# Spreading the row factors of four norms: two one-pass products of their head and rest in place of one fp32 product

## The chip, the cores and the metric

The kernel runs on one core of one Trainium2 chip. The metric is the time of one execution on the device in microseconds (us); the median of three runs is 1458.67 us.

## The reference, cut to what matters

The network has two layers. Each layer normalises the 512 tokens of width 1024, projects them, mixes them in three branches, adds the result, normalises again and runs an MLP; a last norm closes the network.

```python
def rms_norm(x, g):
    xf = x.astype(F32)
    y = xf * lax.rsqrt(jnp.mean(xf * xf, axis=-1, keepdims=True) + EPS)
    return (y * g.astype(F32)).astype(x.dtype)

for l in range(DEPTH):                      # DEPTH = 2
    h = rms_norm(x, norm1_g[l])
    z = h @ w_in[l]
    ...                                     # three branches on slices of z, gated and summed
    x = x + merged @ w_out[l]
    h2 = rms_norm(x, norm2_g[l])
    x = x + jnp.square(jax.nn.relu(h2 @ w_ff1[l])) @ w_ff2[l]
return rms_norm(x, final_norm_g)
```

A row of the norm is multiplied by one factor per token, `rsqrt(mean(x*x) + EPS)`. The kernel does not multiply `h` by it; it multiplies the products of `h` by it later, and for products that have the tokens along the free axis it needs the 512 factors repeated on all 128 partitions.

## The kernel before

Tokens lie in NT = 4 tiles of 128, the width in KB = 8 blocks of 128. Every large product is made of three one-pass fp32r products: head by head, head by rest, rest by head (`mm3`, line 261). Activations in head and rest are `xgh`/`xgl` (after the first norm), `xq`, `xz`, `xy`, `xc` (in the MLP) and `sqh`/`sql` (the MLP's hidden values); weights come by DMA into `raw` (3 buffers), are cast to a head `wh` on ScalarE (ACT) and to a rest `wl` on VectorE (DVE) or on ACT and GpSimd (POOL).

`Norm.stats()` (line 349) makes the factors. From the sums of squares it makes `st_v`, POOL raises it to the power -0.5 into `st_r` (128 x 4: one column for each token tile). Where they are wanted on all partitions (`bc=True`), DVE makes a page `sq` (128 x 512) with four `tensor_scalar` instructions, `ident` times one column of `st_r` each, so four diagonal blocks. TensorE (PE) multiplies a 128 x 128 tile of ones with this page in one fp32 product `statb<-sq,ones` into a PSUM bank; each of its 512 columns then holds a token's factor on every partition. ACT copies the bank into the page `rbc`. Pages of the tag `sq` have two buffers, `rbc` has one.

This happens four times, named here **place 1 to 4**: at the start of layer 0 (line 1091, about 28 us), ahead of the MLP of layer 0 (line 1180, about 413 us), at the start of layer 1 (about 751 us) and ahead of its MLP (about 1127 us). `rbc` is read by DVE: in `s5_u` (line 666, `s5u<-mx,rbc`, the input of one branch, which then goes out to memory and back by the DMAs `bn<-s5u` and `u<-bn` of SP's queue), in `gate_tile` (line 1079), and at the MLP's entry in `fft<-mm,rbc`, which leads over `fft<-fft` to `sqh<-fft` on ACT and `sql<-fft,sqh` on DVE, the operands of the MLP's second product.

The order of instructions on each engine is not written out by hand. The Tile scheduler lays it out with a time simulation of its own at build time (line 1345), under the data dependences, the buffers' turns and some dependences that the kernel adds. An edit that changes a few instructions can so change the order of others around it. Every instruction is recorded at line 110, a wrapper; rows are told apart by the names of their tiles.

Of the kernel before, what the change touches and what calls it, by code (L numbers as in the profile page):

```python
# [10 lines left out]
F32 = dt.float32  # L11
F32R = dt.float32r
AF = mybir.ActivationFunctionType
ALU = mybir.AluOpType

P = 128
# [4 lines left out]
NT = SEQ // P  # L21
# [72 lines left out]
def build(tc, x, positions, norm1_g, w_in, lam_re, lam_im, log_step, b_re, b_im, c_re, c_im, ssm_d,  # L94
# [28 lines left out]
    pe, ve, sc, gp, sy = (Ordered(e) for e in (nc.tensor, nc.vector, nc.scalar, nc.gpsimd, nc.sync))  # L123
    es = contextlib.ExitStack()
    with es:
        cp = es.enter_context(tc.tile_pool(name="cst", bufs=1))
# [3 lines left out]
        def f(t):  # L130
            return t.bitcast(F32)

        def page(dtype=F32, name="pg", tag="pg"):
            t = pool.tile([P, 512], dtype, tag=tag, bufs=BUFS[tag], name=name)
            pending[t.tensor.name] = tag
            return t
# [10 lines left out]
        def small(n, name, bufs=2, dtype=F32):  # L147
            return pool.tile([P, n], dtype, tag=name, bufs=bufs, name=name)
# [4 lines left out]
        def mx_ps(name="mx"):  # L153
            return psp.tile([P, 512], F32, tag="mx", bufs=4, name=name)

        def copy(o, i, scale=1.0):
            sc.activation(o, i, AF.Copy, scale=scale)
# [19 lines left out]
        def cst(n):  # L177
            o, w = COFF[n]
            return ct[:, o:o + w]

        ident, tri, vis, iota, rep32 = (cst(n) for n in ("ident", "tri", "vis", "iota", "rep32"))
        ones = cp.tile([P, P], F32, name="ones")
        gp.memset(ones, 1.0)
        nhalf = cp.tile([P, 16], F32, name="nhalf")
        gp.memset(nhalf, -0.5)
# [112 lines left out]
        class Norm:  # L298
# [50 lines left out]
            def stats(self, bc=True, ts=range(NT)):  # L349
                v = small(NT, "st_v")  # L350
                tt = slice(ts[0], ts[-1] + 1)
                if self.sums is None:
                    ps = mx_ps("stat")
                    for t in ts:
                        pe.matmul(ps[:, 2 * t:2 * t + 2], self.acc[:, t * P:(t + 1) * P], ones[:, 0:2], start=True, stop=True)
                    sums = ps[:, 0:2 * NT].rearrange("p (t a) -> p t a", a=2)[:, tt, 0]
                else:
                    sums = self.sums[:, tt]
                ve.tensor_scalar(v[:, tt], sums, 1.0 / DM, EPS, op0=ALU.mult, op1=ALU.add)
                r = small(NT, "st_r")  # L360
                gp.tensor_tensor(r[:, tt], v[:, tt], nhalf[:, tt], ALU.pow)
                if not bc:
                    return r, None
                dg = page(name="sq", tag="sq")
                for t in range(NT):
                    ve.tensor_scalar(dg[:, t * P:(t + 1) * P], ident, r[:, t:t + 1], None, op0=ALU.mult)
                pb = mx_ps("statb")
                pe.matmul(pb, ones, dg, start=True, stop=True)
                rb = page(name="rbc", tag="rbc")
                copy(rb, pb)  # L370
                return r, rb
# [977 lines left out]
```

## Time and profile before

| | us |
|---|---|
| median of three runs (lowest to highest) | 1458.67 (1458.5 to 1458.79) |
| the profiled execution, its own time | 1458.82 |
| span of the profiled execution | 1456.9 |
| PE busy | 1435.8 |
| DVE busy | 1061.0 |
| ACT busy | 785.1 |
| POOL busy | 176.4 |

The profiled execution's own time is 1.9 us longer than its span, and 0.15 us over the median. The mean granted clock of PE is 0.997 of full speed. A matmul's row gives its start, its length from first column to modelled end, and its operands; neighbouring matmuls overlap, so what one occupies on PE is the distance between the starts, not the length. One fp32 `statb` instruction shows as two records.

### The profile page before, as it was taken

How to read it: one execution, taken by the hardware profiler on the slowest of the kernel's cores; microseconds unless marked ns; L12 is line 12 of the kernel's file. 1: busy time of each engine (PE TensorE's matmuls, PEld its weight loads, DVE VectorE, ACT ScalarE, POOL GpSimd, SP SyncE). 2: the span in 40 equal slices, each digit the busy share in tenths (PEclk: the TensorE clock that was granted, in tenths of full speed). 3: DMA queues.
4: the chain of work that ended last, by engine and by line, in shares of the span. 5: the costliest groups of instructions: out<-in, count | busy, mean ns of one | idle time of the engine just before them, and what ended most of it. 6: DMA issues, size and time to landing. Idle time of an engine off the chain costs nothing.

```text
span 1456.9 us, 22130 instructions
## 1 busy us (share of the span) xinstructions
PE 1435.8 (99%) x8102; PEld 1263.3 (87%) x8102; DVE 1061.0 (73%) x2448; ACT 785.1 (54%) x1224; POOL 176.4 (12%) x247
## 2 busy tenths in 40 slices
PE   8999999999999999999999999999999999999997
PEld 7889898888889889999889889888888999999996
DVE  6966799745877988877576479766477777677754
ACT  5654665663645555555545654566544454545454
POOL 0221121100010011100101112211100000000011
PEclk9999999999999999999999999999999999999999
DMA  7874775846245665655847757768542656565664
GB/s 230 198 151 103 175 174 137 198 102 181 87 113 150 152 155 156 153 144 138 205 148 172 182 125 162 180 140 179 145 149 81 151 153 152 152 152 153 152 162 128
DMA packets 164081, 222.82 MB, mean 153 GB/s; under 512 B 14906, under 2 KB 134532, under 8 KB 163972
## 3 DMA queue, kind: packets, MB, share of 16 engines
q1 hardware_dynamic: 140180, 142.69, 32.2%
q0 software_dynamic: 22464, 76.56, 28.4%
q10 hardware_dynamic: 1328, 2.17, 0.4%
q8 instruction: 63, 1.03, 0.3%
q14 instruction: 46, 0.38, 0.1%
HBM read 136.44 MB, written 8.39 MB: 99 GB/s over the span
## 4 chain that ended last, share of the span: by engine, by line
PE 89%; DMA 5%; issue 3%; DVE 2%; ACT 1%; POOL 0%; SPq 0%; POOLq 0%; ACTq 0%; DVEq 0%
PE mm L110 60%; PE f L110 18%; DMA raw<-in_w_in_dram 2%; DMA wl<-raw 2%; PE yo L110 1%; PE mx L110 1%; PE sp L110 1%; PE pv L110 1%; PE ry L110 1%; PE tr L110 1%; PE pt L110 1%; PE s5y L110 1%; DMA xt<-in_x_dram 1%; DMA raw<-in_w_ff_dram 1%; PE kk L110 0%
## 5 line engine op out<-in xcount | busy, mean ns | idle before, releaser
L110 ACT ACTIVATE wh<-raw 128x1024 fp32r<-128x1024 f32 (+3 forms) x314 | 306.2, 976 | 345.9 <-PE mm L110 219.3
L110 POOL DMA_DIRECT2D wl<-raw x156 | 136.5, 875 | 1002.8 <-ACT wl L110 557.3
L110 DVE TENSOR_TENSOR wl<-raw,wh 128x896 fp32r<-128x896 f32 (+3 forms) x158 | 171.3, 1085 | 92.2 <-ACT wh L110 91.7
L110 PE MATMUL f<-xc,wh 128*128 128x256 f32 x1232 | 224.6, 279 | 0.0
L110 ACT ACTIVATE wl<-raw 128x1024 fp32r<-128x1024 f32 (+1 forms) x156 | 155.6, 998 | 83.4 <-PE mm L110 34.4
L110 PEld LDWEIGHTS f<-xc,wh 128*128 128x128 f32 x1232 | 190.9, 188 | 2.4
L110 PE MATMUL mm<-sql,wh 128*128 128x512 f32 x480 | 188.2, 393 | 0.0
L110 PE MATMUL mm<-sqh,wl 128*128 128x512 f32 x480 | 187.5, 391 | 0.1
L110 PE MATMUL mm<-sqh,wh 128*128 128x512 f32 x480 | 185.1, 391 | 0.0
L110 PE MATMUL f<-xc,wl 128*128 128x256 f32 x616 | 170.3, 279 | 0.0
L110 PE MATMUL mm<-xgh,wh 128*128 128x512 f32 x384 | 151.5, 395 | 1.2 <-ACT zq L110 1.2
L110 PE MATMUL mm<-xgl,wh 128*128 128x512 f32 x384 | 151.7, 395 | 0.0
L110 PE MATMUL mm<-xgh,wl 128*128 128x512 f32 x384 | 151.3, 395 | 0.0
L110 DVE TENSOR_TENSOR raw<-raw 128x256 f32<-128x256 f32 x336 | 107.8, 334 | 52.5 <-DMA raw<-in_w_ff_dram 48.6
L110 PEld LDWEIGHTS f<-xc,wl 128*128 128x128 f32 x616 | 115.4, 188 | 0.5
L110 PE MATMUL mm<-wh,xgh 128*128 128x384 f32 (+1 forms) x320 | 106.1, 336 | 2.7 <-ACT wh L110 1.4
L110 PEld LDWEIGHTS mm<-sqh,wl 128*128 128x128 f32 x480 | 90.2, 188 | 19.6 <-DMA wl<-raw 0.5
L110 PE MATMUL mm<-wl,xgh 128*128 128x384 f32 (+1 forms) x320 | 105.8, 333 | 0.9 <-DVE wl L110 0.7
L110 PEld LDWEIGHTS mm<-sqh,wh 128*128 128x128 f32 x480 | 90.1, 188 | 17.9
L110 PEld LDWEIGHTS mm<-sql,wh 128*128 128x128 f32 x480 | 90.2, 188 | 17.1
L110 PE MATMUL mm<-wh,xgl 128*128 128x384 f32 (+1 forms) x320 | 102.7, 334 | 0.0
L110 DVE TENSOR_TENSOR x<-x,mm 128x512 f32<-128x512 f32 x120 | 80.9, 682 | 9.9 <-PE mm L110 9.9
(405 smaller groups left out, 2865.1 us busy)
## 6 DMA issues: line engine op xcount, KB each, us to landing
wl<-raw POOLq DMA_DIRECT2D x116, 512.0 KB, 5.3
raw<-in_w_ff_dram SPq DMA_DIRECT2D x72, 512.0 KB, 3.5
raw<-in_w_ff_dram SPq DMA_DIRECT2D x112, 256.0 KB, 2.8
raw<-in_w_in_dram SPq DMA_DIRECT2D x52, 512.0 KB, 4.9
wl<-raw POOLq DMA_DIRECT2D x40, 384.0 KB, 4.9
raw<-in_w_in_dram SPq DMA_DIRECT2D x32, 384.0 KB, 3.7
raw<-in_w_out_dram SPq DMA_DIRECT2D x16, 512.0 KB, 3.4
xd<-x SPq DMA_DIRECT2D x16, 256.0 KB, 3.5
```

What stands on the lines that cost most here:

```text
L110: r = fn(*a, **k)
```

## The change

The ones become a tile of type fp32r, and the factors are split on DVE into a head (`st_h`, rounded to fp32r) and a rest (`st_l`). Each part gets a diagonal page of type fp32r, and two one-pass products of the ones with these pages add up in the same PSUM bank.

```diff
-        ones = cp.tile([P, P], F32, name="ones")
+        ones_r = cp.tile([P, P], F32R, name="ones")
+        ones = f(ones_r)
         gp.memset(ones, 1.0)
...
                 if not bc:
                     return r, None
-                dg = page(name="sq", tag="sq")
-                for t in range(NT):
-                    ve.tensor_scalar(dg[:, t * P:(t + 1) * P], ident, r[:, t:t + 1], None, op0=ALU.mult)
+                rh, rl = small(NT, "st_h", 2, F32R), small(NT, "st_l")
+                ve.tensor_copy(rh, r)
+                ve.tensor_tensor(rl, r, f(rh), ALU.subtract)
                 pb = mx_ps("statb")
-                pe.matmul(pb, ones, dg, start=True, stop=True)
+                for n, y in enumerate((f(rh), rl)):
+                    dg = page(F32R, "sq", "sq")
+                    for t in range(NT):
+                        ve.tensor_scalar(dg[:, t * P:(t + 1) * P], ident, y[:, t:t + 1], None, op0=ALU.mult)
+                    pe.matmul(pb, ones_r, dg, start=n == 0, stop=n == 1)
                 rb = page(name="rbc", tag="rbc")
                 copy(rb, pb)
                 return r, rb
```

Over the whole program PE goes from 4 to 8 `statb` products and DVE gets 24 more instructions: 4 casts, 4 subtractions and 16 `tensor_scalar`. ACT, POOL and the DMA queues have the same instructions in number. The scheduler's order differs near the four places only.

On PE at place 1, before: the last products of a group of 128 x 292 outputs, then `statb`, then 48 products into `mx`.

```order
L110 MATMUL mm<-wh,xgl 128x292 [waits DVE_49]
L110 MATMUL mm<-wh,xgl 128x292 x3
L110 MATMUL statb<-sq,ones 128x512 [waits DVE_49,PE_49]
L110 MATMUL mx<-xgh,wh 128x512 [waits PE_49]
L110 MATMUL mx<-xgl,wh 128x512
```

On PE at place 1, now:

```order
L110 MATMUL mm<-wh,xgl 128x292 [waits DVE_49]
L110 MATMUL mm<-wh,xgl 128x292 x3
L110 MATMUL mm<-wh,xgh 128x384 [waits Activation_49]
L110 MATMUL mm<-wh,xgh 128x384 x2
L110 MATMUL statb<-sq,ones 128x512 [waits DVE_49,PE_49]
L110 MATMUL mx<-xgh,wh 128x512 [waits PE_49]
```

Three products of the next group (128 x 384 outputs), which stood behind the 48 of `mx`, now stand ahead of the first `statb`, and they wait for a weight head that ACT casts. The second `statb` stands behind 21 of the 48.

On SP's queue at place 1, before: the branch's input goes out to memory in two halves (`bn`), each read back by four DMAs (`u`), with one weight block (`raw`) ahead of the second four.

```order
L110 DMA bn_99<-s5u 128x512 [waits DMAHW6_49,DVE_49]
L110 DMA u<-bn_99 32x4x128 [waits DMAHW7_49,DMAHW6_49]
L110 DMA u<-bn_99 32x4x128
...
L110 DMA bn_100<-s5u 128x512 [waits DMAHW3_49,DVE_49]
L110 DMA raw<-in_w_in_dram 128x4x256 [waits DMAHW4_49,DVE_49]
L110 DMA u<-bn_100 32x4x128 [waits DMAHW5_49,DMAHW3_49]
```

On SP's queue at place 1, now:

```order
L110 DMA bn_99<-s5u 128x512 [waits DMAHW6_49,DVE_49]
L110 DMA bn_100<-s5u 128x512 [waits DMAHW7_49,DVE_49]
L110 DMA u<-bn_99 32x4x128 [waits DMAHW6_49]
...
L110 DMA u<-bn_100 32x4x128 [waits DMAHW7_49,DMAHW4_49]
L110 DMA u<-bn_100 32x4x128 [waits DMAHW5_49]
L110 DMA u<-bn_100 32x4x128 x2
L110 DMA raw<-in_w_in_dram 128x4x256 [waits DMAHW0_49,DVE_49]
```

The weight block moved behind all eight `u`.

On ACT at place 4 (place 2 reads alike), before: the copy to `rbc`, then the heads `sqh` of the MLP's hidden values in turn with casts of weights.

```order
L110 ACTIVATE rbc<-statb 128x512
L110 ACTIVATE sqh<-fft 128x512
L110 ACTIVATE wh<-raw 128x1024
L110 ACTIVATE sqh<-fft 128x512
L110 ACTIVATE wh<-raw 128x896
L110 ACTIVATE sqh<-fft 128x512
L110 ACTIVATE wh<-raw 128x896
L110 ACTIVATE sqh<-fft 128x512
L110 ACTIVATE wl<-raw 128x1024
```

On ACT at place 4, now:

```order
L110 ACTIVATE rbc<-statb 128x512
L110 ACTIVATE wh<-raw 128x1024
L110 ACTIVATE sqh<-fft 128x512 x2
L110 ACTIVATE wh<-raw 128x896 x2
L110 ACTIVATE wl<-raw 128x1024
L110 ACTIVATE sqh<-fft 128x512 x2
```

The casts of weights moved ahead of the heads: one ahead of the first pair, three ahead of the second.

## Rows read from the trace of the kernel before

**Rows 1.** The page's part 1: busy time, share and instructions of each engine

```profile
PE 1435.8 (99%) x8102; PEld 1263.3 (87%) x8102; DVE 1061.0 (73%) x2448; ACT 785.1 (54%) x1224; POOL 176.4 (12%) x247
```

**Rows 2.** Stretch: us, busy (count) PE PEld DVE ACT POOL, clock, DMA share, GB/s

```profile
745.00:760.00 15.00, 15.00 (x83) 13.06 (x84) 9.66 (x47) 5.95 (x12) 1.04 (x1) 1.00 0.37 104
1120.00:1142.00 22.00, 22.00 (x122) 18.79 (x121) 16.36 (x33) 9.46 (x12) 3.22 (x3) 1.00 0.42 112
```

**Rows 3.** Timeline of PE at place 1: start us, us, instruction, [idle before]

```profile
26.80 0.80 PE L110 MATMUL mm<-wh,xgl 128*128 128x292 f32 x4
27.68 1.10 PE L110 MATMUL statb<-sq,ones 128*128 128x512 f32 x2
...
28.85 0.40 PE L110 MATMUL mx<-xgl,wh 128*128 128x512 f32 x1
```

**Rows 4.** Timeline of PE 30 us later

```profile
57.48 0.34 PE L110 MATMUL mm<-wh,xgl 128*128 128x384 f32 x1
59.04 0.50 PE L110 MATMUL mm<-xgh,wh 128*128 128x512 f32 x1 [1.23 <-ACT zq L110]
```

**Rows 5.** The chain that ended last, in order of time, up to 59 us

```profile
43.16 3.52 DMA raw<-in_w_in_dram
...
49.91 7.53 DMA raw<-in_w_in_dram
```

**Rows 6.** Timeline of PE at place 4

```profile
1127.02 0.62 PE L110 MATMUL mm<-xc,wh 128*128 128x512 f32 x2
1127.48 1.02 PE L110 MATMUL statb<-sq,ones 128*128 128x512 f32 x2
...
1128.57 0.62 PE L110 MATMUL mm<-xc,wh 128*128 128x512 f32 x2
```

**Rows 7.** The tile statb: duration in ns min/median/max, first and last start

```profile
L110 PE MATMUL statb<-sq,ones x8: 590/592/667, 27.7 to 1127.9; 128*128 128x512 f32 x8
```

**Rows 8.** Timeline of DVE at place 4 and behind it

```profile
1122.14 0.87 DVE L110 TENSOR_SCALAR sq<-ct,st_r 128x128 f32<-128x128 f32 x4
1125.11 1.08 DVE L110 TENSOR_TENSOR raw<-raw 128x256 f32<-128x256 f32 x3 [2.09 <-DMA raw<-in_w_ff_dram]
...
1129.17 1.29 DVE L110 TENSOR_TENSOR fft<-mm,rbc 128x512 f32<-128x512 f32 x2 [1.42 <-ACT rbc L110]
```

**Rows 9.** Timeline of DVE elsewhere: a small cast to fp32r

```profile
43.02 0.17 DVE L110 CAST p_rh<-p_th 128x16 fp32r<-128x16 f32 x1
```

**Rows 10.** Timeline of ACT behind place 4

```profile
1137.06 0.96 ACT L110 ACTIVATE wh<-raw 128x896 fp32r<-128x896 f32 x1 [0.99 <-ACT sqh L110]
1137.92 0.61 ACT L110 ACTIVATE sqh<-fft 128x512 fp32r<-128x512 f32 x1
```

**Rows 11.** Timeline of PE where the MLP's second product starts

```profile
1136.93 0.39 PE L110 MATMUL mm<-sqh,wh 128*128 128x512 f32 x1
...
1140.14 0.73 PE L110 MATMUL f<-xc,wh 128*128 128x256 f32 x5
1140.71 0.39 PE L110 MATMUL f<-xc,wl 128*128 128x256 f32 x2
```

**Rows 12.** Timeline of ACT at place 1

```profile
28.48 0.86 ACT L110 ACTIVATE wh<-raw 128x768 fp32r<-128x768 f32 x1
```

**Rows 13.** Timeline of SP's queue behind place 1 (time at the queue's head)

```profile
42.68 0.38 SPq L110 DMA_DIRECT2D bn<-s5u  x1
43.16 0.40 SPq L110 DMA_DIRECT2D raw<-in_w_in_dram  x1
45.34 1.74 SPq L110 DMA_DIRECT2D u<-bn  x4
```

**Rows 14.** Busy time by stretch in the first 61 us (columns as Rows 2)

```profile
8.34:11.75 3.41, 1.87 (x12) 1.38 (x12) 2.52 (x4) 3.41 (x9) 0.00 (x0) 1.00 0.94 335
11.75:15.16 3.41, 3.41 (x16) 3.41 (x16) 2.47 (x6) 3.41 (x10) 0.00 (x0) 0.50 0.33 81
...
57.00:60.50 3.50, 2.27 (x11) 1.73 (x10) 2.21 (x12) 2.48 (x4) 1.36 (x3) 1.00 0.95 225
```

## The prediction

> **What bounds the kernel now.** I read the page's busy times first: PE is busy 1435.8 of 1456.9 us, DVE 1061.0, ACT 785.1 [rows 1]. So PE's sequence sets the time, and a change counts by what PE occupies and by where PE comes to wait. The table by stretch shows it at the places: PE is busy 15.00 of 15.00 us round place 3 and 22.00 of 22.00 round place 4, DVE 9.66 and 16.36, the DMA engines 0.37 and 0.42 [rows 2]. Place 2 has the same pattern as place 4, so its rows are not shown. Place 1, at 27.68 [rows 3], is different. It lies in the first 60 us, where PE meets weights that have just come. There PE waits 1.23 us at 59.04 for ACT's `zq` [rows 4]; the chain of work shows that a weight block issued at 49.91 and landing 7.53 us later, at 57.44, stands behind that wait, and before it another that SP issued at 43.16 [rows 5].
>
> **What the products save.** At place 4 two one-pass products of 128 x 512 start at 1127.02 and what follows starts at 1127.48, so one occupies 0.46 / 2 = 0.23 us of PE. From the start of `statb` at 1127.48 to 1128.57 lie the fp32 product and one such one-pass product: 1.09 us, so the fp32 product occupies 1.09 - 0.23 = 0.86 us [rows 6]. Two one-pass products occupy 0.46. Each place saves 0.40 us, four places 1.60. The eight records of `statb` last 590 to 667 ns with a median of 592, so the four places are alike [rows 7]; at place 1 the distance is 28.85 - 27.68 - 0.23 = 0.94, because PE waits a little inside it [rows 3].
>
> A rule of the Trainium skill would give a little more. "FP8 and Floating Point Precision", section TensorE Precision Notes, says that true fp32 takes four passes through the array. By it the old product would occupy 4 x 0.23 = 0.92 us, an estimate, each place would save 0.46, and the four 1.84 in place of 1.60; the row of place 4 has 0.86, and I go by the row.
>
> **What DVE pays at places 2, 3 and 4.** The four `tensor_scalar` of one diagonal take 0.87 us [rows 8]. The added diagonal costs that again, and the cast and the subtraction (128 x 4) at most the 0.17 us each that a cast of 128 x 16 lasts [rows 9]: at most 0.87 + 0.34 = 1.21 us a place. At place 4 DVE next waits 2.09 us for a DMA [rows 8], and at place 2 as well, so the addition lies wholly in that wait; without it, it would delay weight rests by 1.2 us. At place 3 no such single wait follows, but DVE is busy only 9.66 of 15.00 us in that stretch [rows 2], and the second `statb` stands ten products (2.3 us) behind the first, more than its diagonal takes. So on PE's path the split costs nothing at these places. The extremes are nothing and 1.2 us a place.
>
> **What comes later behind places 2 and 4.** Now `statb` ends later: its head stands two products later in PE's row than the old one did, two more stand between the two. From the old start the new pair ends after 2 + 1 + 2 + 1 = 6 one-pass products, 1.37 us, against 0.86: `rbc` comes 0.5 us later. DVE already waits 1.42 us for it [rows 8], so `fft` comes 0.5 us later as well. Ahead of the second pair of heads `sqh` ACT now has two casts `wh` and one `wl`. In the old order the last of these `sqh` starts at 1137.92 behind a `wh` of 0.96 us [rows 10]; in the new order I put the third `sqh` at 1138.4 to 1139.0, by setting the same durations one behind another, and its rest `sql` ending near 1141.2. PE starts the MLP's second product at 1136.93, now with twelve products (12 x 0.23 = 2.8 us) and then some twenty of 0.114 us each (five from 1140.14 to 1140.71) ahead of the third `sqh` [rows 11]. So PE wants the third `sqh` near 1136.9 - 0.4 + 2.8 + 2.3 = 1141.6 and its `sql` near 1142.9: 1.7 us of cover or more. I take -0.40 at each of places 2, 3 and 4, together -1.2.
>
> **What place 1 costs.** Here the order moves. Three products of 128 x 384 now stand ahead of the first `statb`, and they need a head `wh` that ACT casts from 28.48 for 0.86 us, so to 29.34 [rows 12]. The four products that stand ahead end at 26.80 + 0.80 = 27.60 [rows 3]. So PE gets a new wait of about 1.7 us. What it gets back: 29.34 + 3 x 0.17 + 0.23 is 30.1 for the first `mx`, against 28.62 before (28.85 - 0.23); the second `statb` adds 0.23 later, the three products fall out where they stood (-0.52). PE then runs 30.1 - 28.6 + 0.2 - 0.5 = 1.2 us late when it comes to the wait at 59.04. That wait holds 1.23 us. If only PE were late it would vanish in it almost wholly. But that wait ends by a DMA, and SP's row changed too: the weight block that went out at 43.16 now stands behind eight `u`. The second `bn` can leave 1 us or so before its old 42.68 plus the 1.2 by which PE is late; its `u` started 2.66 us after it and took 1.74 [rows 13]; so the block leaves near 46.7, 3.5 us late, and the four small loads and the block of 49.91 behind it nearly at their old time, 0 to 0.3 late. The late block then shares the DMA engines with that one. It took 3.52 us [rows 5], so it overlaps the other's first microsecond, and I let the block that lands at 57.44 land 0.3 to 1.5 us later. The wait at 59.04 ends that much later. The middle, +0.9, is my value for place 1, in place of -0.40; the ends are 0 (both late parts hidden) and +3.5 (the whole lateness of the block carried on).
>
> **The sum.** -1.2 + 0.9 = -0.3 us on the profiled execution's own 1458.82 (span 1456.9 and 1.9 round it): 1458.5. That execution is 0.15 over the median, so against the median the forecast is 1458.4.
>
> **The rivals.**
> 1. *The whole gain.* Place 1 costs nothing and saves its 0.40: the new wait vanishes in the one at 59.04 and the block lands in time. For it: that wait is 1.23 us long and PE is 1.2 late. Against it: the wait is set by a DMA, and the block ahead of it leaves 3.5 us later. Time: 1458.67 - 1.6 = 1457.1.
> 2. *The casts go first.* Behind places 2 and 4 the moved casts make ACT late with the second pair of `sqh`, as the casts themselves wait for weights, and PE waits. It decides from 1.7 us of lateness on. At 2.7 us PE loses 1.0 twice: -1.2 + 0.9 + 2.0 = +1.7, or 1460.4. Against it: the last `wh` of the old order started at 1137.06 and had waited for an `sqh`, not for a load [rows 10].
> 3. *The late block, and a slow clock behind it.* The whole 3.5 us of the block's lateness reaches the landing at 57.44, PE idles 3.5 us longer behind 57.65, and its granted clock falls. What a fall costs is in the first 16 us: PE was busy 1.87 of 3.41 us, and in the next 3.41 us the granted clock was 0.50 (1.2 in place of 2.4 GHz) [rows 14], half of the work of that stretch, 1.7 us. Time: -1.2 + 3.5 + 1.7 = +4.0, or 1462.7, slower. It decides where the lateness passes 2.4 us. Against it: round the wait of 1.23 us, from 57 to 60.5, the clock stayed full [rows 14], and SP's later loads hardly move. The Trainium skill ("TensorE: Matmul & The Clock Gate", Part 1) says that an idle array is throttled and that activity releases it; the row at 11.75 agrees.
> 4. *No saving.* A one-pass product with ones of type fp32r, standing alone between others, occupies as much as half the fp32 one (0.43). Then only place 1's cost is left: +0.9, or 1459.6. Against it: the products round it are one-pass, of the same size, at 0.23.
>
> **How the numbers follow.** Forecast 0.60 (1457.9 to 1459.1 by its own bounds of 0.3 and 1.5), whole gain 0.17, casts 0.08, late block 0.10, no saving 0.05. The range from 1456.9 to 1460.5 takes in all but the late block, and what lies beyond the sums. 0.2% is 2.9 us, about what a measurement of this kernel can tell from no change; only the late block passes it upward (0.10), and no row gives a gain of that size: -1.6 with the whole wait of 1.23 gone is 2.8. I leave 0.03 for it, taken from the forecast's part; 0.87 is left for no change.
>
> **What would show it.** Two `statb` records of one pass each, with 0.23 us between neighbours; PE waiting about 1.7 us for ACT's `wh` near 27.6; SP's block of 43.16 near 46.7; the wait for `zq` ending near 59.9; PE without a wait at places 2 to 4, `rbc` 0.5 us later there. The forecast is wrong if PE waits for `sqh` or `sql` behind place 2 or 4, if the clock falls behind 29 or 59 us, or if the block lands later than 59.8.

## The result, and the profile after

The changed kernel takes 1471.10 us (median of six runs, 1469.41 to 1476.49) against 1458.73 before: 12.4 us more, a ratio of 1.0086 with a 95% interval of 1.0072 to 1.0100. The forecast was 1458.4 with a range from 1456.9 to 1460.5. The profiled execution took 1471.95 us, with a span of 1470.2 against 1456.9: 13.3 us more.

Part 1 of the page of the changed kernel answers to [rows 1]:

```profile
PE 1448.2 (99%) x8102; PEld 1264.5 (86%) x8102; DVE 1065.1 (72%) x2472; ACT 785.1 (53%) x1224; POOL 176.1 (12%) x247
```

This is the first thing to see. The change takes work from PE, yet PE is busy 12.4 us longer with the same number of records. DVE got 24 instructions and 4.1 us, ACT nothing. So most of the loss is not waiting: PE's own products take longer. The table of waits of PE in the changed kernel (what it waited for, us in total, times, longest) has nothing that could hold 13 us:

```profile
PE mm L110 <- ACT wh L110: 3.1, 3, 1.8
PE mm L110 <- ACT zq L110: 1.8, 1, 1.8
PE pv L110 <- ACT ph L110: 1.4, 2, 1.2
```

The chain that ended last (the work followed back from the last instruction, each step to what released it) shows where it is. It has long pieces in which PE does nothing but one-pass products of 512 columns, none with a wait. Here are two such pieces (start us, us, what, number of products) of the kernel before, then the same two of the changed one:

```profile
331.41 71.16 PE mm L110 x309
...
1043.75 73.32 PE mm L110 x320
```

```profile
336.86 72.32 PE mm L110 x309
...
1053.50 74.54 PE mm L110 x320
```

The same 320 products take 73.32 us before and 74.54 after: 0.2291 and 0.2329 us for one. Nothing in these pieces was edited, no order in them changed, and they lie far from the four places. When the starts of equal products are laid side by side, the distance grows from +3.4 us at 59.04 to +13.3 at the end, steadily wherever there are products of 512 columns. By the names of their tiles 3,480 of them grew so (those with `xgh`, `sqh`, `mh` and other early pages as the operand of 512 columns, called the moving one below); at 3.8 ns each they are 13.2 us.

The second, smaller loss is at place 1. Timeline of PE (start us, us, instruction, idle before), answering to [rows 3] and [rows 4]:

```profile
26.70 0.69 PE L110 MATMUL mm<-wh,xgl 128*128 128x292 f32 x4
29.18 0.79 PE L110 MATMUL mm<-wh,xgh 128*128 128x384 f32 x3 [1.78 <-ACT wh L110]
29.80 0.39 PE L110 MATMUL statb<-sq,ones 128*128 128x512 f32 x1
30.03 0.43 PE L110 MATMUL mx<-xgh,wh 128*128 128x512 f32 x1
```

Stretches of the same kernel around it (columns as in [rows 2], granted clock third from the end):

```profile
26.85:30.26 3.41, 1.63 (x10) 1.32 (x9) 3.41 (x16) 3.14 (x6) 0.00 (x0) 1.00 0.71 237
30.26:33.67 3.41, 3.41 (x9) 2.66 (x8) 3.41 (x22) 0.56 (x1) 0.00 (x0) 0.50 0.61 181
```

PE waits 1.78 us for the weight head; then its clock is granted at half, 1.2 GHz, for 3.41 us. SP's queue and the chain answer to [rows 13] and [rows 5]:

```profile
41.86 2.84 SPq L110 DMA_DIRECT2D bn<-s5u  x2
44.75 4.86 SPq L110 DMA_DIRECT2D u<-bn  x8
49.70 0.40 SPq L110 DMA_DIRECT2D raw<-in_w_in_dram  x1
```

```profile
54.88 5.92 DMA raw<-in_w_in_dram
60.82 1.06 ACT wl L110
61.88 0.48 ACT zq L110
62.35 0.04 issue
62.40 3.76 PE mm L110 x15
```

The block that went out at 43.16 now goes at 49.70, the one of 49.91 at 54.88, and PE resumes at 62.40 in place of 59.04: place 1 costs 3.4 us in this pair of profiles. The old time at this point is not a firm one. In the nine other kernels below whose place 1 is that of before, the same product starts anywhere from 56.86 to 59.49, after a wait of 0 to 1.09 us in place of 1.23. One of them is the kernel whose first place keeps its old product (e3 below):

```profile
58.00 0.50 PE L110 MATMUL mm<-xgh,wh 128*128 128x512 f32 x1
```

### The profile page after: what moved, and what is told of

It reads as the page before. It is cut to its first block, busy times and chain, and to the rows that moved or that the text cites. A ratio compares the mean times of both kernels' runs of the same rounds, so it can differ in the third digit from the quotient of the medians.

```text
span 1470.2 us, 22144 instructions
## 1 busy us (share of the span) xinstructions
PE 1448.2 (99%) x8102; PEld 1264.5 (86%) x8102; DVE 1065.1 (72%) x2472; ACT 785.1 (53%) x1224; POOL 176.1 (12%) x247
## 4 chain that ended last, share of the span: by engine, by line
PE 94%; DMA 2%; ACT 1%; DVE 1%; issue 0%; SPq 0%; POOL 0%; POOLq 0%; ACTq 0%; DVEq 0%
PE mm L110 65%; PE f L110 19%; PE mx L110 2%; PE yo L110 1%; PE sp L110 1%; PE tr L110 1%; PE pv L110 1%; PE ry L110 1%; PE pt L110 1%; DMA raw<-in_w_in_dram 1%; DMA xt<-in_x_dram 1%; PE s5y L110 1%; PE kk L110 0%; DMA wl<-raw 0%; PE rs L110 0%
```

## The experiments

The theories:

- **A, where the weights lie.** The change needs four small tiles (two buffers each of `st_h` and `st_l`, 128 bytes a partition in all), and in the built program's memory layout they stand between the activation pages and `rbc`. All that comes behind, `rbc`, `raw`, `wh`, `wl` among it, lies 128 bytes higher in SBUF (on-chip memory); the pages that hold `xgh`, `sqh` or `mh` don't move. The start of a page is 32 past a multiple of 256 in both kernels; the start of a weight tile is 224 past one before and 96 past one after. By A the distance between the moving operand (512 columns, here a page) and the stationary one (128 x 128, here weights) sets what a product occupies. Distances are taken modulo 256 bytes, in the texts below "in a raster of 256": 192 before, 64 in the changed kernel.
- **B.** The loss spreads from place 1 through later order and buffers.
- **C.** The fp32r ones or the split itself make products slower.

### A hole of 128 bytes in the kernel before (e1)

```diff
+                pool.tile([P, 32], F32, tag="pad", bufs=1, name="pad")
                 pb = mx_ps("statb")
                 pe.matmul(pb, ones, dg, start=True, stop=True)
```

> The kernel before, with one unused tile of 128 bytes a partition set between the pages and rbc, so that the weight tiles wh and wl (and raw, z0, qT behind them) lie 128 bytes higher, as they do in the changed kernel; every engine's order is that of before. Theory A (where the weights lie against the moving pages sets what a 512-column product occupies): products of 512 columns go from 0.229 to 0.233 us, some 2,300 of them, so about +9.4 us: 1468. Theory B (the loss spreads from place 1, its wait, clock and moved loads): 1458.7, nothing moves. Theory C (the fp32r ones or the split itself slow the products): 1458.7.

Measured: 1471.73 us, a ratio of 1.0090 (1.0077 to 1.0103). The tile is never written or read, and every engine has its instructions in the order of before. Part 1 of its page, and the same two pieces of the chain:

```profile
PE 1449.9 (99%) x8102; PEld 1264.9 (86%) x8102; DVE 1061.9 (72%) x2448; ACT 785.4 (53%) x1224; POOL 178.2 (12%) x247
```

```profile
333.68 72.35 PE mm L110 x309
...
1051.89 74.54 PE mm L110 x320
```

The 320 products take the 74.54 us of the changed kernel to the hundredth. 128 unused bytes make a loss as large as the whole one, with nothing of the change in the kernel: B and C fall as its cause. My size was too small, since I had counted 2,300 products in place of 3,480.

### The same hole in the changed kernel: 256 bytes in all (e2)

```diff
                 ve.tensor_tensor(rl, r, f(rh), ALU.subtract)
+                pool.tile([P, 32], F32, tag="pad", bufs=1, name="pad")
                 pb = mx_ps("statb")
```

> The changed kernel with the same unused 128 bytes, so that the weights lie 256 bytes higher than before, the same place in a raster of 256. Order as in the changed kernel. Theory A: products back at 0.229 us, the time 1471.1 - 9.4 = 1461.7, of which place 1 keeps its loss of about 3.4 and the other three places give back 0.4 each. Theory B and C: 1471, as the changed kernel.

Measured: 1460.90 us, a ratio of 1.0014 (1.0000 to 1.0028) to before. The chain:

```profile
334.85 71.18 PE mm L110 x309
...
1046.42 73.32 PE mm L110 x320
```

With the old distance the old 73.32 us is back, and 10 of the 12 us, while the split is still in the kernel. What is left, 2.1 us, fits place 1's loss less the savings of the others.

### Place 1 as before, the other three split (e3)

The weights lie 256 bytes higher, as in the last one.

```diff
-            r, rb = nrm.stats()
+            r, rb = nrm.stats(plain=l == 0)
...
+                if plain:
+                    dg = page(name="sq", tag="sq")
+                    for t in range(NT):
+                        ve.tensor_scalar(dg[:, t * P:(t + 1) * P], ident, r[:, t:t + 1], None, op0=ALU.mult)
+                    pe.matmul(pb, ones, dg, start=True, stop=True)
+                else:
...
```

> As the kernel of e2 (weights 256 bytes higher), but place 1 keeps its one fp32 product; only places 2, 3 and 4 are split. Theory A: products at 0.229 us, place 1 as before, so only the three savings of 0.40 are left: 1458.7 - 1.2 = 1457.5. Theory B: 1458 or so too, as place 1 is undisturbed. Theory C: 1468, the products stay at 0.233.

Measured: 1458.83 us, a ratio of 1.0007 (0.9995 to 1.0019): no difference from before that can be told, so 1457.5 was neither seen nor excluded. Against e2, whose edit differs at place 1 alone, it is 2.1 us faster in the medians of twelve runs each. The trace tells more than the times do. Laid beside the kernel before, its products start 0.34 us late ahead of place 3 and 0.06 early behind it: -0.40, the term of the sum. Around place 4 it is 0.14 early and then 0.53, or -0.39, and around place 2 it is 0.44 late and then 0.06, or -0.38. At places 2 and 4 a tenth is given back in the next 20 us. PE at place 4, answering to [rows 6]:

```profile
1127.57 0.39 PE L110 MATMUL mm<-xc,wh 128*128 128x512 f32 x1
1127.80 0.39 PE L110 MATMUL statb<-sq,ones 128*128 128x512 f32 x1
1128.03 0.40 PE L110 MATMUL mm<-xc,wh 128*128 128x512 f32 x1
1128.27 0.39 PE L110 MATMUL mm<-xc,wl 128*128 128x512 f32 x1
1128.50 0.39 PE L110 MATMUL statb<-sq,ones 128*128 128x512 f32 x1
1128.73 0.63 PE L110 MATMUL mm<-xc,wh 128*128 128x512 f32 x2
```

Each `statb` occupies 0.23 us, the pair 0.46 in place of 0.86. PE waits for nothing between 1110 and 1160.

### A hole of 192 bytes (e4)

```diff
+                pool.tile([P, 48], F32, tag="pad", bufs=1, name="pad")
                 pb = mx_ps("statb")
```

> The kernel before with an unused tile of 192 bytes: the weights' distance from the moving pages in a raster of 256 is 128, which neither kernel has. Theory A: another value than one of 0.229 or 0.233 us is possible; by the two distances seen slow (0 and 64) and the one seen fast (192) I expect one of the two, 1458.7 or 1468. Theory B and C: 1458.7.

Measured: 1476.52 us, a ratio of 1.0121 (1.0106 to 1.0135), slower than the slow value I allowed. Its row in the chain, and the costliest group of products of 256 columns (count, then busy us and mean ns), this kernel's and that of the kernel before:

```profile
1054.35 74.30 PE mm L110 x320
```

```profile
L110 PE MATMUL f<-xc,wh 128*128 128x256 f32 x1232 | 228.7, 282 | 0.0
```

```profile
L110 PE MATMUL f<-xc,wh 128*128 128x256 f32 x1232 | 224.6, 279 | 0.0
```

At this distance the products of 256 columns take longer as well, which they don't with 128 bytes (225.2).

### Place 1 with PE's old row (e5)

All four places are split, with 256 bytes; the first products of the 128 x 384 group are held behind the second `statb`.

```diff
+                    self.spread = pe.matmul(pb, ones_r, dg, start=n == 0, stop=n == 1).ins.name
...
-                        mm3(pss[t][:, :n], nrm.h[k][:, c], nrm.l[k][:, c], wh, wl, k == 0, k == KB - 1)
+                        mm3(pss[t][:, :n], nrm.h[k][:, c], nrm.l[k][:, c], wh, wl, k == 0, k == KB - 1, after if k == 0 else None)
...
-                dsa_q(l, od, tm_group(l, C_DQ, 384, nrm, mm_ps), r)
+                dsa_q(l, od, tm_group(l, C_DQ, 384, nrm, mm_ps, after=nrm.spread), r)
```

> As the kernel of e2 (all four places split, weights 256 bytes higher), but the first products of the 128x384 group are held behind the second statb of place 1, so that PE's row at place 1 reads as before. SP's row stays as in the changed kernel: the weight block behind all eight reads u. Theory P (place 1's loss is PE's new wait for the weight head and the slow clock behind it): no wait near 27.5, no stretch at half clock, the loss of 3.4 us gone, 1457.5. Theory S (it is the weight block that SP sends 3.5 us later): the loss stays, 1460.9 as e2.

Measured: 1460.28 us, a ratio of 1.0010 (0.9997 to 1.0023). Neither theory holds as written. The wait for the weight head is gone, but another stands in its place (PE, then DVE):

```profile
29.02 0.47 PE L110 MATMUL statb<-sq,ones 128*128 128x512 f32 x1 [2.09 <-DVE sq L110]
```

```profile
26.80 1.22 DVE L110 TENSOR_TENSOR wl<-raw,wh 128x1024 fp32r<-128x1024 f32 x1
27.93 0.16 DVE L110 TENSOR_TENSOR st_l<-st_r,st_h 128x4 f32<-128x4 f32 x1
28.01 0.87 DVE L110 TENSOR_SCALAR sq<-ct,st_h 128x128 fp32r<-128x128 f32 x4
```

The scheduler has put the head's diagonal behind a weight rest on DVE, so `statb` waits 2.09 us. The granted clock fell here too (0.50 from 30.35 to 33.76). The resuming product that started at 59.04 before starts at 61.01, 2.0 us late in place of e2's 3.6 at the same product. That may be PE's row, but the two figures differ by less than the 2.6 us by which this product's start differs among kernels with the old place 1, and the medians (1460.28 and 1460.90) cannot be told apart. So what PE's row, DVE and SP each add to place 1's loss is not shown.

### All tiles 32 bytes higher (e6)

```diff
+        cp.tile([P, 8], F32, name="pad0")
         ct = cp.tile([P, CONSTS.shape[1]], F32, name="ct")
```

> The kernel before with 32 unused bytes a partition at the very start, so that all tiles lie 32 bytes higher: the distance of weights and moving pages is as before, their place against multiples of 64 is not. Theory A1 (the distance between the two operands counts): 0.229 us, 1458.7. Theory A2 (each operand's own place against a raster counts): another value, by up to the 0.004 us seen, or more.

Measured: 1458.89 us, a ratio of 1.0000 (0.9986 to 1.0013). Its chain:

```profile
1044.09 73.32 PE mm L110 x320
```

Pages and weights both lie elsewhere against multiples of 64, their distance is as before, and the products are too: A1.

### Holes of 32, 96, 160 and 224 bytes (e7, e8, e10, e11)

The edit is that of the hole of 192, with another width.

> The kernel before with an unused tile of 32 bytes ahead of rbc: weights start at a multiple of 256, moving pages stay at 32 past one, distance 224. Theory A1: a value of its own, between 0.229 and 0.234 us by the four distances seen, 1458.7 to 1472. Theory A2 with the weights' own place counting: the weights now lie on a multiple of 64, 0.229 or less.

> The kernel before with an unused tile of 96 bytes ahead of rbc: weights 64 past a multiple of 256, distance 32 in a raster of 256. Theory A1: slow as the distances 0 and 64 beside it, 0.233 us, 1468 to 1472. Theory A2 with the weights' own place counting: as e7, since both lie on a multiple of 64.

> The kernel before with an unused tile of 160 bytes ahead of rbc: distance of weights from moving pages 96 in a raster of 256, not seen so far. Theory A1: slow like the five other distances that are not 192, 0.233 us, 1470; a distance that is faster than 192 is not excluded.

> The kernel before with an unused tile of 224 bytes ahead of rbc: distance 160 in a raster of 256, the last one not seen. Theory A1: slow, 0.233 us, 1470; a distance that is faster than 192 is not excluded.

Measured, one run each: 1469.48, 1470.56, 1477.46 and 1475.26 us. With single runs the products' rows carry the reading, more than the times. Rows of the chain in this order:

```profile
1050.12 74.54 PE mm L110 x320
```

```profile
1051.52 74.55 PE mm L110 x320
```

```profile
1056.01 74.83 PE mm L110 x320
```

```profile
1053.71 74.56 PE mm L110 x320
```

With 32 bytes the weights start at a multiple of 256, as they do in e6; here a product takes 0.2329 us and there 0.2291. So the weights' own place does not decide. Nor does that of the moving pages, which is the same in the kernel before and with every hole. A2 falls.

All kernels together, by the distance from the start of a moving page to that of a weight tile, modulo 256:

| distance | kernel | 320 products, us | one, us |
|---|---|---|---|
| 192 | before; all 32 higher; split with 256 | 73.32 | 0.2291 |
| 224 | hole 32 | 74.54 | 0.2329 |
| 32 | hole 96 | 74.55 | 0.2330 |
| 64 | hole 128; the changed kernel | 74.54 | 0.2329 |
| 96 | hole 160 | 74.83 | 0.2338 |
| 128 | hole 192 | 74.30 | 0.2322 |
| 160 | hole 224 | 74.56 | 0.2330 |

The last column is the mean of the 320; 38 of them have a moving tile that lies behind the weights and keep their distance, so the others differ from 0.2291 by a little more. Of the seven distances one is fast, and the kernel before has it. The distance 0 was not set by a kernel (a few products within the kernels, such as those with `xz`, lie at it), and steps finer than 32 bytes were not run. No distance run is faster than 192.

### The hole behind the weights (e9)

```diff
+            pool.tile([P, 32], F32, tag="pad", bufs=1, name="pad")
             z = pool.tile([P, NT, N_G0], F32, tag="z0", bufs=1, name="z0")
```

> The kernel before with the unused 128 bytes set behind the weight tiles instead of ahead of them: raw, wh and wl stay where they were, all later tiles lie 128 bytes higher as in the changed kernel, xq, xz and xy among them, which are the moving side of some 158 products. Theory A1 (distance between moving and stationary operand): the products with xgh, xgl, sqh, sql, mh, ml stay at 0.229 us, only those 158 go to 0.233: +0.6 us, 1459.5. Theory D (a hole anywhere, or the place of later tiles, costs): 1470 as the hole of 128 ahead of the weights.

Measured: 1461.16 us against 1460.54 of before beside it, a ratio of 1.0002 (0.9981 to 1.0024). Its chain:

```profile
1044.82 73.38 PE mm L110 x320
```

The same 128 bytes cost nothing that can be measured where they don't come between the pages and the weights. Over the trace the products whose moving side is an early page keep 0.229 us, and those with `xc`, `xq` or `xy`, which moved with the hole (168 by the traces, where I had counted 158 with `xz`), go from 0.230 to 0.232. In the changed kernel it is the other way round: those tiles lie behind the weights, moved with them, and their products stay at 0.230, while the rest went to 0.233. So within one kernel, too, it is the distance that tells the products apart.

The last product of the program, `yo`, shows the same from the other side. There the weights are the moving operand and `sqh` or `sql` the stationary one, so the distance is 64 in the kernel before and 192 in the changed one. Its row in the chain of the kernel before, then of the changed one:

```profile
1431.15 15.41 PE yo L110 x66
```

```profile
1444.70 15.14 PE yo L110 x66
```

That is 0.2335 and 0.2294 us for one: where the products with early pages as the moving operand became slower, these became faster. They take 15.14 us in the two kernels whose weights lie 128 bytes higher (e1 and the changed one) and 15.35 to 15.48 in the eleven others.

## Why the prediction was wrong

- **The step that failed** is the first sentence of its method: that a change counts by what PE occupies at the places and where it waits. The sum took the 0.23 us of a neighbouring one-pass product as given for all the others. It has no term for 3,480 products elsewhere, and that term, 3.8 ns for each, is as large as the whole loss: the hole alone costs 12.9 us. The built program's memory layout shows that the weights move by 128 bytes, and the prediction compared the order of instructions and not the layout. The trace of before holds a hint: its `yo` products, which lie at the distance of 64 that the change gives to the others, take 0.2335 us beside 0.2291.
- **What the products save** was right: 0.40 a place, measured 0.38, 0.40 and 0.39 at places 2 to 4 in e3's profile, with a tenth given back behind 2 and 4.
- **What DVE pays, and what comes later** was right. Timeline of DVE of the changed kernel at place 4, answering to [rows 8]:

```profile
1133.37 0.87 DVE L110 TENSOR_SCALAR sq<-ct,st_h 128x128 fp32r<-128x128 f32 x4
1134.15 0.87 DVE L110 TENSOR_SCALAR sq<-ct,st_l 128x128 fp32r<-128x128 f32 x4
1135.94 1.08 DVE L110 TENSOR_TENSOR raw<-raw 128x256 f32<-128x256 f32 x3 [0.91 <-DMA raw<-in_w_ff_dram]
...
1140.68 1.29 DVE L110 TENSOR_TENSOR fft<-mm,rbc 128x512 f32<-128x512 f32 x2 [1.97 <-ACT rbc L110]
```

  The wait for the DMA shrank from 2.09 to 0.91 us and holds the addition of 1.2 us; the wait for `rbc` grew by 0.55 (0.5 forecast). PE did not wait for `sqh` or `sql`.
- **Place 1** was mis-sized, too: +0.9 taken, +3.4 in the changed kernel's profile and 2.1 in the medians of e2 against e3. Even with the old distance the kernel takes 1460.90 us, just above the range. The wait of 1.7 us came (1.78). Two things were not in the value. The clock fell right behind that wait, at 30.26, and not at 59 as the rival had it; 3.41 us at a granted clock of 0.50 are 1.7 us. And SP's blocks left at 49.70 and 54.88 where I had 46.7 (my own terms, 42.68 - 1 + 1.2 + 2.66 + 1.74, give 47.3) and 49.9 to 50.2: with PE later, `s5u` and `bn` are later, `u` follows, and the four small loads then waited in the queue as well. The landing was 3.4 us late, beyond the 2.4 from which rival 3 was to decide. So rival 3 had both parts, the lateness and the slow clock, but not as a sum: the slow stretch came ahead of the wait for the late block, so its 1.7 us do not come on top of the 3.4, where the rival adds 3.5 and 1.7 to 5.2. Its total with the three savings, +4.0, stands against the 2.1 of e2. The 1.23 us in which my value hid PE's lateness were a single profile's, too: in the nine other profiles with the old place 1 that wait is 0 to 1.09 us.
- **Rival 4** (no saving) and **rival 2** (casts) fell; rival 1 did, too, by place 1.
- Whether the losses simply add is not shown. The hole alone costs 12.9 us, place 1 less the savings 2.1 (e2), both together 12.4 and not 15.0; but the intervals of the three are each some 2 us to either side, so the gap of 2.6 may be noise. A slower PE may also meet weights that have come, so that some of its waits shrink; that was not tried.

## What to carry to other kernels

A new small tile can cost more than the instructions that fill it: here it moved every tile behind it, and with them the distance between the two operands of thousands of products. So compare the memory layout, and not only the order, before and after an edit, and put a new tile where it doesn't come between the two, or fill up to the old distance. When PE is busy longer with the same records, take a long piece of like products in the chain of both traces and divide: a change of 1.7% in one product showed there at once, while the table of waits stayed silent. And before a term rests on one wait, read that wait in several profiles with the same order: the one at 59.04 was 1.23 us in one and nothing in others.

## What the runs showed of the hardware that I had not expected

- One product of 128 x 512 occupies, in the mean of 320, 0.2291 us at a distance of 192 (modulo 256) between its moving page and its weights, and 0.2322 to 0.2338 at the six other distances run. Moving both together by 32 bytes changes nothing. Products with the weights as the moving operand follow the same distance (`yo`: 0.2335 at 64, 0.2294 at 192). What in the chip makes the difference, and whether the weights of this product or of the next one count, was not tried.
- PE's clock was granted at half for one stretch of 3.41 us at least once in every profile, not always behind a wait. In the hole of 128 bytes it fell at 98.92, behind a stretch in which PE was busy all the time:

```profile
95.51:98.92 3.41, 3.41 (x33) 3.41 (x33) 0.00 (x0) 2.77 (x5) 0.86 (x1) 1.00 0.84 166
98.92:102.33 3.41, 3.41 (x18) 3.41 (x18) 0.80 (x3) 1.34 (x5) 0.18 (x1) 0.50 0.98 203
```

  In all three kernels with a wait of about 2 us at place 1 it fell right behind that wait.
